# Strassen's algorithm on all columns of the down projection in groups 0 to 6 of an encoder's MLP

## The chip, the cores and the metric

The kernel runs on one core of a Trainium2 chip. The metric is the device time of one execution in microseconds; for the kernel before three runs gave 2014.59 to 2015.04, median 2015.0. Engines are named as the profile names them: PE is TensorE (PEld its weight loads), DVE is VectorE, ACT is ScalarE, POOL is GpSimd, SP is SyncE, whose queue issues the loads.

## The reference

Two layers of an encoder on 256 tokens of width 2048, all in float32. Each layer is RMSNorm, three attention mixers over one input projection, an output projection with residual, and then the part that the change touches, a squared-ReLU MLP of inner width 8192:

```python
for l in range(DEPTH):                       # DEPTH = 2
    ...                                      # mixers, output projection, residual
    h = rmsnorm(x, norm_mlp[l])
    u = jax.nn.relu(jnp.einsum('bsd,df->bsf', h, w_up[l]))        # 256 x 8192
    x = x + jnp.einsum('bsf,fd->bsd', u * u, w_down[l])           # 256 x 2048
return rmsnorm(x, norm_final)
```

## The kernel before, in words

**Numbers.** A float32 operand is split into a hi part (rounded to the matmul's input format, float32r) and a lo part (the rest). A product is hi x hi + lo x hi + hi x lo: three matmuls of 128 x 128 weights by 512 columns for each pair of blocks. The tiles of B that a step multiplies with are split on the way: ScalarE casts the hi tile (line 988, `whi`), VectorE subtracts it from the raw tile for the lo (line 989, `wlo`). There are three hi and three lo buffers, and two more (`spare`) that serve as a fourth hi and lo tile in some stages and hold B11 in the MLP.

**Steps.** All of the work on weights is one list of steps. A step has a tile of weights of 512 KB (1024 columns on 128 partitions), its load (issued 7 steps ahead, `LOOK_LOAD`), its split (2 or 3 steps ahead), sometimes sums of weight tiles (`prep`, 5 steps ahead), and its matmuls. A scheduler then puts the instructions of each engine in one fixed order, in which each waits for its operands, so that an instruction that waits holds up all that stand behind it on its engine.

**The MLP.** The 8192 rows of w_down are 8 groups of 1024. While group g goes down, group g+1 comes up: 16 up steps (4 blocks q of 4 steps, 8 matmuls of 512 columns and 8 of 256 each, lines 691 and 696). After each block, an evacuation (lines 668 to 676) adds halves, applies ReLU, scale and square, and splits the result; `sums_of` (lines 712 to 717) makes the sums of A that Strassen's products need.

**Strassen.** In groups 0 to 6 the left 1024 columns of w_down go by Strassen's algorithm in Winograd's form: A (the 256 tokens by 1024 rows) and B (1024 rows by 1024 columns) are 2 x 2 blocks, and seven products P1 to P7 take the place of eight. Each product is two steps of 6 matmuls (line 802), one for each half h of its rows. The products P1, P6, P5, P3 gather in bank a and P7, P4 in bank d of one pair tile `S` of PSUM, P2 in a bank of its own; after each product its bank is added to or subtracted from x (line 782). The sums of B that P6, P7 and P4 need are made by VectorE (lines 815, 817, 821, 832): 8 a group. The other 1024 columns go by plain steps of 12 matmuls (line 477), 8 a group, evacuated by line 739; group 7 is plain throughout. Between the two steps of a product stands an up or plain step, and between two products stand two or three.

Of the kernel before, what the change touches and what calls it, by code (L numbers as in the profile page):

```python
# [43 lines left out]
def tile_trunk(ctx: ExitStack, tc: tile.TileContext, x_in, w_in, w_o, w_up, w_down,  # L44
               gains, rowp, t5, rpb, gfin, cst, onehot, out):
    nc = tc.nc
    LOOK_LOAD, LOOK_SPLIT, LOOK_PREP, BUDGET = 7, 2, 5, 2.2
# [417 lines left out]
    class Step:  # L465


        def __init__(self, src, kk, n, pre, mm, fourth=True, loads=None, prep=None, raw=None, post=None):
            self.src, self.kk, self.n, self.pre, self.mm, self.fourth = src, kk, n, pre, mm, fourth
            self.loads, self.prep, self.raw, self.post = loads or [], prep, raw, post  # L470
# [33 lines left out]
    def layer_steps(l):  # L504
# [152 lines left out]
        def up_steps(g):  # L657

            out_, evacs = [], []
            for q in range(4 * g, 4 * g + 4):  # L660
                box = {}

                def evac(q=q, box=box):
                    need(("rrow", l))
                    a = mid(F32, 2, 256)
                    for i in range(2):

                        nc.scalar.copy(a[:, i, :], box["b"][i][:, 256:512])
                        nc.vector.tensor_add(a[:, i, :], a[:, i, :], box["b"][i][:, 0:256])
# [11 lines left out]
                for s in range(4):  # L681
# [19 lines left out]
                    out_.append(Step(w_up[l, q * 4 + s], 4, 256, pre, mm, fourth=False,  # L701
# [5 lines left out]
        def sums_of(q, a):  # L707
# [3 lines left out]
            a11, a21, a12 = v[:, 0, :], v[:, 1, :], v[:, 2, :]  # L711
            nc.vector.tensor_sub(sm[:, 0:2, :], v[:, 0:4:3, :], v[:, 1:2, :].to_broadcast([P, 2, P]))
            nc.vector.scalar_tensor_tensor(sm[:, 2, :], sm[:, 1, :], -1.0, a11, op0=ALU.mult, op1=ALU.subtract)
# [6 lines left out]
        def down_steps(g, js):  # L720
            out_ = []
            for j in js:
                box = {}
                for k in range(4):
                    def mm(wh, wl, j=j, k=k, box=box):
                        if k == 0:
# [3 lines left out]
                        hts = [uT[4 * g + k]] * 2  # L730
                        mode_b(box["b"], hts, wh, wl, [0, 1], k == 0, k == 3, blocks=(0,) if final else (0, 1),
                               lo_last=g < 7)
# [7 lines left out]
                        if final:  # L740
# [3 lines left out]
                            for c in range(2):  # L744
                                cols = slice(c * 256, c * 256 + 256)
                                for i, (hts, vh, vl) in enumerate(box["w"]):
                                    mode_b([None, tail[c]], hts, vh[:, :, cols], vl[:, :, cols], [0, 1],
                                           i == 0, i == 3, n=256, blocks=(1,))
# [9 lines left out]
                    out_.append(Step(w_down[l, (g * 4 + j) * 4 + k], 2, 512, None, mm, fourth=g == 7))  # L758
            return out_

        def strassen_steps(g):
# [5 lines left out]
            raw, t2, box = {}, {}, {}  # L767

            def src(par, j, h):
                return w_down[l, g * 16 + (par * 2 + j) * 2 + h]  # L770

            def left(name, q):

                if name[0] == "A":
                    t, kk = int(name[1]) - 1, int(name[2]) - 1
                    return [uT[q][:, i, kk, t * P:(t + 1) * P] for i in range(2)]
                return [sT[q][:, i, "3124".index(name[1]), :] for i in range(2)]

            def evac(bank, t, j, sign):
                xs = x[:, t, j * 512:(j + 1) * 512]  # L780
# [4 lines left out]
            plan = [("P1", "A11", "a", True, (0, 0, 1)), ("P6", "S2", "a", False, (1, 0, 1)),  # L785
                    ("P7", "S3", "d", True, (1, 1, -1)), ("P5", "S1", "a", False, (1, 1, -1)),
                    ("P3", "S4", "a", False, (0, 1, -1)), ("P2", "A12", "b", True, (0, 0, 1)),
                    ("P4", "A22", "d", False, (1, 0, 1))]
            out_ = []
            for name, lf, bk, fresh, dst in plan:  # L790
                for h in range(2):
                    def mm(wh, wl, name=name, lf=lf, bk=bk, fresh=fresh, dst=dst, h=h):
# [3 lines left out]
                        if (name, h) == ("P2", 0):  # L796
                            box["b"] = mm_bank()
                        o = box[bk]
                        ops = [left(lf, 2 * h + i + 4 * g) for i in range(2)]
                        for a, w in ((0, wh), (1, wh), (0, wl)):  # L800
                            for i in range(2):
                                nc.tensor.matmul(o, ops[i][a], w[:, i, :], skip_group_check=True,  # L802
                                                 start=fresh and h == 0 and i == 0 and a == 0 and w is wh,
                                                 stop=h == 1 and i == 1 and w is wl)
                        if h == 1:
# [369 lines left out]
```

## Time and profile before

| | |
|---|---|
| median of 3 runs | 2015.0 us (2014.59 to 2015.04) |
| the profiled execution | 2015.19 us, span 2013.4 us, mean clock 0.999 |
| busy: PE, DVE, ACT, POOL | 2000.6 us (99%), 1618.2 (80%), 1200.9 (60%), 290.6 (14%) |
| loads of w_down | 144 plain (`wraw`), 84 to `side`, 28 to `spare`, 512 KB each |
| transfer engines | 59.8% of their time on the loads' queue, mean 191 GB/s |

The profile is a record of one execution. A busy share is a mean over stages, and the MLP is about two thirds of the span, so the tables by stretches are read for it. A row of the timeline has the start, the duration, the engine, the line of the kernel, and tiles written <- tiles read. Durations of instructions that follow each other overlap a little, so the pace is read from their starts.

### The profile page before, as it was taken

The numbers are of one execution on the slowest core, as the hardware profiler recorded it, in microseconds if no ns is written. First come the engines' busy times: TensorE is split into PE (matmuls) and PEld (weight loads), VectorE is DVE, ScalarE is ACT, GpSimd is POOL, SyncE is SP. The second block draws the span as 40 slices with busy tenths as digits, with TensorE's granted clock in tenths as the row PEclk, the third lists the DMA queues.
The fourth block names the chain that finished last, engine by engine and source line by source line (L and its number), as shares of the span: only waits on it lengthen the run. The fifth ranks groups of instructions, "written<-read, shape, count | busy, mean of one in ns | idle before, by whom it ended". The sixth has DMA issues, their size and how long they took to land.

```text
span 2013.4 us, 27963 instructions
## 1 busy us (share of the span) xinstructions
PE 2000.6 (99%) x10264; PEld 1706.0 (85%) x10264; DVE 1618.2 (80%) x2112; ACT 1200.9 (60%) x1732; POOL 290.6 (14%) x336
## 2 busy tenths in 40 slices
PE   9999999999999999999999999999999999999998
PEld 7888888888888888888888888888888888888887
DVE  6677877879888898887657688778888888888875
ACT  6667756565555556555656677565655556555554
POOL 0684520000000000000008745100000000000001
PEclk9999999999999999999999999999999999999999
DMA  7745655565575656656666456555665756657554
GB/s 276 226 154 162 209 170 190 168 217 193 178 228 170 219 184 192 215 172 198 189 184 200 152 176 198 176 189 179 192 215 170 231 167 210 205 169 233 166 167 156
DMA packets 110102, 384.97 MB, mean 191 GB/s; under 512 B 12515, under 2 KB 16867, under 8 KB 109964
## 3 DMA queue, kind: packets, MB, share of 16 engines
q1 hardware_dynamic: 109532, 382.08, 59.8%
q8 instruction: 81, 1.33, 0.3%
q10 hardware_dynamic: 432, 1.10, 0.2%
q14 instruction: 57, 0.47, 0.1%
HBM read 377.34 MB, written 2.11 MB: 188 GB/s over the span
## 4 chain that ended last, share of the span: by engine, by line
PE 98%; ACT 1%; DVE 0%; issue 0%; DMA 0%; SPq 0%; DVEq 0%; POOLq 0%; POOL 0%
PE mm L477 44%; PE mm L691 23%; PE mm L696 12%; PE S L802 11%; PE mm L802 2%; PE tr L392 1%; PE tr L411 1%; PE S L355 1%; PE S L354 1%; PE tr L221 1%; PE tr L404 0%; ACT big L372 0%; PE tr L267 0%; DMA x<-in_x_dram 0%; PE tr L283 0%
## 5 line engine op out<-in xcount | busy, mean ns | idle before, releaser
L989 DVE TENSOR_TENSOR wlo<-wraw,whi 128x1024 fp32r<-128x1024 f32 (+1 forms) x531 | 654.6, 1236 | 212.5 <-ACT whi L988 209.9
L988 ACT CAST whi<-wraw 128x1024 fp32r<-128x1024 f32 (+1 forms) x531 | 556.7, 1051 | 418.1 <-PE mm L691 170.2
L477 PE MATMUL mm<-whi,big 128*128 128x512 f32 (+1 forms) x2252 | 643.8, 386 | 0.5 <-ACT whi L988 0.5
L691 PE MATMUL mm<-big,whi 128*128 128x512 f32 x2048 | 509.5, 391 | 0.0
L477 PEld LDWEIGHTS mm<-whi,big 128*128 128x128 f32 x2252 | 418.6, 188 | 83.5 <-ACT whi L988 2.5
L691 PEld LDWEIGHTS mm<-big,whi 128*128 128x128 f32 x2048 | 377.1, 188 | 74.1
L477 PE MATMUL mm<-wlo,big 128*128 128x512 f32 (+1 forms) x1126 | 374.9, 384 | 0.0
L696 PEld LDWEIGHTS mm<-big,wlo 128*128 128x128 f32 x2048 | 279.4, 190 | 20.0
L696 PE MATMUL mm<-big,wlo 128*128 128x256 f32 x2048 | 285.5, 282 | 0.0
L477 PEld LDWEIGHTS mm<-wlo,big 128*128 128x128 f32 x1126 | 211.8, 188 | 39.6
L802 PE MATMUL S<-whi,big 128*128 128x512 f32 x672 | 182.2, 393 | 0.0
L477 PE MATMUL mm<-spare,big 128*128 128x512 f32 (+1 forms) x678 | 157.8, 381 | 0.0
L988 ACT CAST whi<-side 128x1024 fp32r<-128x1024 f32 x84 | 88.2, 1050 | 95.2 <-PE mm L691 77.8
L477 PEld LDWEIGHTS mm<-spare,big 128*128 128x128 f32 x678 | 122.3, 188 | 23.2
L802 PEld LDWEIGHTS S<-whi,big 128*128 128x128 f32 x672 | 119.1, 189 | 18.7
L989 DVE TENSOR_TENSOR wlo<-side,whi 128x1024 fp32r<-128x1024 f32 x84 | 102.7, 1223 | 37.5 <-ACT whi L988 37.1
L257 POOL TENSOR_TENSOR sm<-sm,mhalf 128x2 f32<-128x2 f32 (+2 forms) x14 | 15.3, 1092 | 793.7 <-DVE sm L252 773.9
L988 ACT CAST whi<-big 128x1024 fp32r<-128x1024 f32 x56 | 59.0, 1053 | 85.1 <-DVE big L817 36.4
L870 POOL TENSOR_TENSOR x<-x,big 128x512 f32<-128x512 f32 x6 | 8.6, 1451 | 669.5 <-ACT mid L877 669.5
L802 PE MATMUL S<-wlo,big 128*128 128x512 f32 x336 | 103.9, 390 | 0.0
L383 POOL TENSOR_SCALAR big<-big,sm 128x256 f32<-128x256 f32 x128 | 90.3, 723 | 3.0
L989 DVE TENSOR_TENSOR spare<-wraw,spare 128x1024 fp32r<-128x1024 f32 x54 | 70.2, 1299 | 22.2 <-ACT spare L988 21.7
(151 smaller groups left out, 2081.3 us busy)
## 6 DMA issues: line engine op xcount, KB each, us to landing
wraw<-in_w_up_dram SPq DMA_DIRECT2D x256, 512.0 KB, 4.1
wraw<-in_w_down_dram SPq DMA_DIRECT2D x144, 512.0 KB, 3.7
wraw<-in_w_in_dram SPq DMA_DIRECT2D x119, 512.0 KB, 3.8
side<-in_w_down_dram SPq DMA_DIRECT2D x84, 512.0 KB, 4.2
wraw<-in_w_o_dram SPq DMA_DIRECT2D x64, 512.0 KB, 3.6
spare<-in_w_down_dram SPq DMA_DIRECT2D x28, 512.0 KB, 4.2
side<-in_rpb_dram SPq DMA_DIRECT2D x32, 174.8 KB, 5.1
side<-avec SPq DMA_DIRECT2D x8, 384.0 KB, 5.4
```

The source lines that it names most:

```text
L221: tr = nc.tensor.transpose(psv[:, kk, t, :], x[:, t, c0:c0 + P], ident).ins
L354: nc.tensor.matmul(o, st, u.kh[:, kh, :], start=True, stop=False)
L355: nc.tensor.matmul(o, st, u.kl[:, kh, :], start=False, stop=True)
L383: nc.gpsimd.tensor_scalar(p[:, s, :], p[:, s, :], rs[:, s:s + 1], 1.0, op0=ALU.mult, op1=ALU.mult)
L392: nc.tensor.transpose(ps[:, c * P:(c + 1) * P], u.p[:, s, kb * P:(kb + 1) * P], ident)
L411: nc.tensor.matmul(ps, u.V[:, kb, u.kv, :, :], pt[:, kb, :], start=n == 0, stop=n == 3)
L477: return nc.tensor.matmul(banks[t][:, 0:n], a, (wl if part == "hl" else wh)[:, i, :], start=first and i == 0 and part == "hh", stop=last a ...
L691: nc.tensor.matmul(box["b"][fs], wh[:, kk, fs * P:(fs + 1) * P], ht, start=s == 0 and kk == 0, stop=False, skip_group_check=True)
L696: nc.tensor.matmul(box["b"][fs][:, 0:256], wl[:, kk, fs * P:(fs + 1) * P], ht[:, 0:256], start=False, stop=s == 3 and kk == 3, skip_group_ ...
L802: nc.tensor.matmul(o, ops[i][a], w[:, i, :], skip_group_check=True, start=fresh and h == 0 and i == 0 and a == 0 and w is wh, stop=h == 1 ...
L988: act = nc.scalar.copy(h[:, part], w[:, part]).ins
L989: last_lo[0] = nc.vector.tensor_sub(lo[:, part], w[:, part], f(h[:, part])).ins
```

## The change

All 2048 columns of groups 0 to 6 go by Strassen's algorithm, as two halves of 1024. A half has 14 steps of 6 matmuls, so a group has 28 of them and 16 up steps, with no plain step. The order of steps is one Strassen step, one up step, one Strassen step for each product, with two up steps ahead of a group and one more between the halves.

- The order of products is P1, P2, P7, P6, P5, P3, P4. P2 of each half has a PSUM bank of its own for the whole layer (`own`), gathers over the groups and is evacuated after group 6 alone.
- B11 is loaded into a plain buffer (`wraw`, five of them) and stays there. B12 is then added onto it by an accumulating transfer from GpSimd's queue (`on_top`, line 796), where VectorE added before; B21 is added onto t2 in the same way. B21 itself is the plain load of P2's step. VectorE keeps two sums for each half of rows: B12 + B22 (line 828) and t2 = B22 + B11 (line 833).
- The `spare` tiles are the fourth hi and lo tile in all stages (every fourth step), and up and Strassen steps are split up to 3 steps ahead (`ahead=4`), the others 1.
- The evacuation of an up block writes its halves in another order, so that the three blocks of A that the products use as they are lie side by side, and 384 columns are split where 512 were.

```diff
-        def __init__(self, src, kk, n, pre, mm, fourth=True, loads=None, prep=None, raw=None, post=None):
+        def __init__(self, src, kk, n, pre, mm, ahead=2, loads=None, prep=None, raw=None, post=None):
...
-                    u = big(F32R, 2, 2, 256)
-                    nc.scalar.copy(u[:, 0], a)
-                    nc.vector.tensor_sub(u[:, 1], a, f(u[:, 0]))
+                    u = big(F32R, 2, 512)
+                    n, af = 384 if q < 28 else 512, a.rearrange("p k c -> p (k c)")
+                    nc.scalar.copy(u[:, 0, 0:n], af[:, 0:n])
+                    nc.vector.tensor_sub(u[:, 1, 0:n], af[:, 0:n], f(u[:, 0, 0:n]))
...
-            plan = [("P1", "A11", "a", True, (0, 0, 1)), ("P6", "S2", "a", False, (1, 0, 1)),
-                    ("P7", "S3", "d", True, (1, 1, -1)), ("P5", "S1", "a", False, (1, 1, -1)),
-                    ("P3", "S4", "a", False, (0, 1, -1)), ("P2", "A12", "b", True, (0, 0, 1)),
+            plan = [("P1", "A11", "a", True, (0, 0, 1)), ("P2", "A12", "b", True, (0, 0, 1)),
+                    ("P7", "S3", "d", True, (1, 1, -1)), ("P6", "S2", "a", False, (1, 0, 1)),
+                    ("P5", "S1", "a", False, (1, 1, -1)), ("P3", "S4", "a", False, (0, 1, -1)),
                     ("P4", "A22", "d", False, (1, 0, 1))]
+
+            def on_top(tile, par, j, h):
+                nc.gpsimd.dma_start(tile, src(par, j, h).rearrange("p (k n) -> p k n", k=2), accum_op=ALU.add)
...
-                        if h == 1:
+                        if h == 1 and (bk != "b" or g == 6):
                             evac(o, *dst)
                     loads, prep, get = [], None, None
                     if name == "P1":
-                        loads = [(("B11", h), src(0, 0, h), lambda h=h: spare(F32, h))]
+                        loads = [(("B11", h), src(0, 0, h), lambda: wp.tile([P, 2, 512], F32, tag="wraw", bufs=5, name=nm("b11")))]
                         get = lambda h=h: raw["B11", h]
+                    elif name == "P2":
+                        def prep(h=h):
+                            assert ("P1", h) in done
+                            on_top(raw["B11", h], 0, 1, h)
...
                         def prep(h=h):
-                            nc.vector.tensor_add(raw["B11", h], raw["B11", h], raw["B12", h])
                             t2[h] = big(F32, 2, 512)
                             nc.vector.tensor_add(t2[h], raw["B22", h], raw["B11", h])
                         get = lambda h=h: t2[h]
...
+                    elif name == "P5":
+                        def prep(h=h):
+                            assert ("P6", h) in done
+                            on_top(t2[h], 1, 0, h)
                         get = lambda h=h: raw["B11", h]
...
-            ss = down_steps(g, (2, 3)) + up_steps(g + 1)
-            hs = strassen_steps(g)
+            ss = up_steps(g + 1)
+            hs = strassen_steps(g, 0) + strassen_steps(g, 1)
             order = [0, 0]
-            for p_ in range(7):
-                order += [1, 0, 1] + ([0, 0] + [0] * (p_ in (1, 3, 5)) if p_ < 6 else [])
+            for p_ in range(14):
+                order += [1, 0, 1] + [0] * (p_ == 6) if p_ < 13 else [1, 1]
...
-        if s.fourth and fourth[0] % 4 == 0:
+        if i % 4 == 3:
...
-        while ns < min(len(steps), i + LOOK_SPLIT + (not s.fourth)):
+        while ns < min(len(steps), i + s.ahead):
```

What this makes of each engine's order is shown at two places. First PE, at the end of one product and the start of the next that waits for an evacuation, in a middle group of the first layer. Before, P7's last step (`S_4610`) and the start of the two up steps that stand between it and P5, whose first row waits for P7's evacuation:

```order
L802 MATMUL S_4610<-whi_4799,big_4416 128x512
L802 MATMUL S_4610<-whi_4799,big_4548 128x512
L802 MATMUL S_4610<-wlo_4800,big_4416 128x512 [waits DVE_49]
L802 MATMUL S_4610<-wlo_4800,big_4548 128x512
L691 MATMUL mm_4779<-big_3321,whi_4809 128x512 [waits Activation_49]
L691 MATMUL mm_4780<-big_3321,whi_4809 128x512
```

Now, in the second half of a group (`S_7353`), P7's last step (`whi_7449`) and P6's first (`whi_7461`):

```order
L810 MATMUL S_7353<-whi_7449,big_6870 128x512
L810 MATMUL S_7353<-wlo_7450,big_6672 128x512 [waits DVE_49]
L810 MATMUL S_7353<-wlo_7450,big_6870 128x512
L810 MATMUL S_7353<-whi_7461,big_6285 128x512 [waits DVE_49,Activation_49]
L810 MATMUL S_7353<-whi_7461,big_6483 128x512
L810 MATMUL S_7353<-whi_7461,big_6285 128x512
L810 MATMUL S_7353<-whi_7461,big_6483 128x512
L693 MATMUL mm_7479<-big_3237,whi_7473 128x512 [waits Activation_49]
```

The first row of P6 waits for VectorE, and the instruction that it waits for is P7's evacuation; nothing stands between the two products any more.

Second VectorE at the same two places. Before, the evacuation (L782) of P7 and what stands ahead of it:

```order
L989 TENSOR_TENSOR wlo_4776<-wraw_4706,whi_4775 128x1024 [waits DMAHW6_49,Activation_49]
L832 TENSOR_TENSOR big_4626<-side_4992,big_4626 128x1024 [waits DMAHW3_49]
L989 TENSOR_TENSOR wlo_4800<-side_4617,whi_4799 128x1024 [waits PE_49,Activation_49]
L989 TENSOR_TENSOR wlo_4810<-wraw_4736,whi_4809 128x1024 [waits DMAHW7_49,PE_49,Activation_49]
L989 TENSOR_TENSOR wlo_4832<-wraw_4754,whi_4831 128x1024 [waits DMAHW0_49,PE_49,Activation_49]
L832 TENSOR_TENSOR big_4660<-side_5043,big_4660 128x1024 [waits DMAHW5_49]
L782 TENSOR_TENSOR x<-x,S_4610 128x512 [waits PE_49]
L989 TENSOR_TENSOR wlo_4845<-spare_4478,whi_4844 128x1024 [waits Activation_49]
```

Now, from the evacuation of an up block (`mid_7432`) to P7's (L786) and the lo tile of P6's first step (`wlo_7462`):

```order
L669 TENSOR_TENSOR mid_7432<-mid_7432,mm_7292 128x256 [waits Activation_49]
L670 SCALAR_TENSOR_TENSOR mid_7432<-mid_7432,rrow 128x512 [waits DVE_49]
L714 TENSOR_TENSOR mid_7442<-mid_7432 128x256 [waits Activation_49]
L715 SCALAR_TENSOR_TENSOR mid_7442<-mid_7442,mid_7432 128x128 [waits DVE_49]
L678 TENSOR_TENSOR big_7439<-mid_7432,big_7439 128x384 [waits Activation_49]
L716 SCALAR_TENSOR_TENSOR mid_7442<-mid_7442,mid_7432 128x128 [waits DVE_49]
L828 TENSOR_TENSOR side_7732<-side_7732,side_7734 128x1024 [waits DMAHW6_49,DMAHW0_49]
L719 TENSOR_TENSOR big_7446<-mid_7442,big_7446 128x512 [waits Activation_49]
L833 TENSOR_TENSOR big_7453<-side_7347,b_1416_7221 128x1024 [waits DMASW4_49]
L833 TENSOR_TENSOR big_7477<-side_7385,b_1426_7273 128x1024 [waits DMASW5_49]
L786 TENSOR_TENSOR x<-x,S_7353 128x512 [waits PE_49]
L1002 TENSOR_TENSOR wlo_7462<-big_7453,whi_7461 128x1024 [waits Activation_49]
```

The rows ahead of the evacuation were lo tiles for steps further on and sums for P4; now the sums for P6 (L833, which wait for the accumulating transfers, `DMASW`) and a sum for the next half's P7 (L828) stand ahead of the evacuation.

More of the change, by code (lines that the diff above doesn't have):

```diff
@@ L699, in mm @@
                             evac()
-                    out_.append(Step(w_up[l, q * 4 + s], 4, 256, pre, mm, fourth=False,
+                    out_.append(Step(w_up[l, q * 4 + s], 4, 256, pre, mm, ahead=4,
                                      post=evacs[0] if (q, s) == (1, 0) else None))
@@ L718, in sums_of, with down_steps @@
             sT[q] = t
-        def down_steps(g, js):
+        def down_steps(g):
             out_ = []
-            for j in js:
+            for j in range(4):
                 box = {}
```

83 lines of the change are left out of this document (40 added, 43 removed).

## The prediction

> **What bounds the kernel now.** I read the page's busy shares and the chain that ended last, then one group of the MLP in the table by stretches, then the timelines of TensorE, VectorE and ScalarE inside a group, and last the landing times of transfers.
>
> ```profile
> PE 2000.6 (99%) x10264; PEld 1706.0 (85%) x10264; DVE 1618.2 (80%) x2112; ACT 1200.9 (60%) x1732; POOL 290.6 (14%) x336
> ...
> PE 98%; ACT 1%; DVE 0%; issue 0%; DMA 0%; SPq 0%; DVEq 0%; POOLq 0%; POOL 0%
> ```
>
> TensorE (PE) is the bound: it is never idle and holds 98% of the chain. Shares over the whole kernel hide the stage that changes, so here are two groups, cut from the first matmul of the same Strassen product in one group to that in the next:
>
> ```profile
> core 0: us, PE busy (x) PEld busy (x) DVE busy (x) ACT busy (x) POOL busy (x), PEclk, DMA share, GB/s
> 530.37:615.87 85.50, 85.50 (x439) 73.12 (x438) 73.67 (x89) 49.16 (x59) 0.00 (x0) 1.00 0.62 197
> 615.87:701.36 85.49, 85.49 (x439) 73.11 (x437) 73.68 (x89) 49.16 (x59) 0.00 (x0) 1.00 0.61 197
> ```
>
> A group lasts 85.5 us, and VectorE (DVE) works 73.7 of them. So a group has 11.8 us of VectorE slack, and that is the stock from which this change pays. The clock is granted in full, GpSimd (POOL) does nothing there.
>
> **What PE saves.** The pace of its steps, by starts in the timeline:
>
> ```profile
> 736.86 1.09 PE L802 MATMUL S<-whi,big 128*128 128x512 f32 x4
> 737.79 0.62 PE L802 MATMUL S<-wlo,big 128*128 128x512 f32 x2
> 738.25 1.98 PE L691 MATMUL mm<-big,whi 128*128 128x512 f32 x8
> 740.07 1.12 PE L696 MATMUL mm<-big,wlo 128*128 128x256 f32 x8
> 741.02 1.09 PE L802 MATMUL S<-whi,big 128*128 128x512 f32 x4
> ...
> 742.40 1.98 PE L691 MATMUL mm<-big,whi 128*128 128x512 f32 x8
> 744.22 1.12 PE L696 MATMUL mm<-big,wlo 128*128 128x256 f32 x8
> 745.17 2.00 PE L691 MATMUL mm<-big,whi 128*128 128x512 f32 x8
> ```
>
> A Strassen step (6 matmuls) takes 738.25 - 736.86 = 1.39 us, an up step 745.17 - 742.40 = 2.77 us. The changed group has 28 Strassen and 16 up steps: 28 x 1.39 + 16 x 2.77 = 83.2 us, 2.3 less than 85.5. By matmuls it is 12 fewer a group, and a plain step of 12 without a seam takes 2.72 us:
>
> ```profile
> 1006.86 2.88 PE L477 MATMUL mm<-spare,big 128*128 128x512 f32 x12
> 1009.58 0.39 PE L477 MATMUL mm<-whi,big 128*128 128x512 f32 x1
> ```
>
> Over 14 groups that is 32 to 38 us; I take 35.
>
> **What VectorE gains in work.** Its pace, by starts where it did not wait:
>
> ```profile
> 706.98 0.75 DVE L669 TENSOR_TENSOR mid<-mid,mm 128x256 f32<-128x256 f32 x2
> 707.64 0.68 DVE L782 TENSOR_TENSOR x<-x,S 128x512 f32<-128x512 f32 x1
> 708.24 0.69 DVE L670 SCALAR_TENSOR_TENSOR mid<-mid,rrow 128x512 f32<-128x512 f32 x1
> ...
> 711.88 0.42 DVE L712 TENSOR_TENSOR mid<-mid 128x256 f32<-128x256 f32 x1
> 712.22 1.22 DVE L815 TENSOR_TENSOR spare<-spare,side 128x1024 f32<-128x1024 f32 x1
> 713.35 0.29 DVE L713 SCALAR_TENSOR_TENSOR mid<-mid,mid 128x128 f32<-128x128 f32 x1
> 713.55 1.22 DVE L989 TENSOR_TENSOR wlo<-spare,whi 128x1024 fp32r<-128x1024 f32 x1
> 714.69 0.28 DVE L714 SCALAR_TENSOR_TENSOR mid<-mid,mid 128x128 f32<-128x128 f32 x1
> ```
>
> So 1024 columns take 1.14 us, 512 take 0.60, 256 take 0.33, 128 take 0.20; 384 is then about 0.47. A group's lo subtractions go from 38 to 44 (+6.8 us), its evacuations into x from 11 to 12 (+0.6; P2 stays in its own bank until group 6), its sums of B stay at 8 (two halves would need 16, but 8 are now accumulating transfers), and four up evacuations split 384 columns for 512 (-0.5). VectorE needs 73.7 + 6.9 = 80.6 us in a group of 83.2: its slack shrinks from 11.8 to 2.6 us. ScalarE gets 6 casts more, about 6 us on 49.2: no bound.
>
> **Where it hits.** An average of 97% leaves no room for a local heap, and the order has one. Before, the shortest PE work between a product's last matmul and the next one that waits for its evacuation is 5.4 us (two plain steps), everywhere. Now it is 2.8 us or less at most such places, and none at all where P6 follows P7 in the second half (12 of the 14 groups); there P6 waits for P7's evacuation although it writes the other bank of the pair, as the row of P6 in the built order says. I walk VectorE's queue there, from the end of the up step that stands ahead of P2's second step (0 us). PE has P2, P7, up, P7: 3 x 1.39 + 2.77 = 6.94 us until P6. VectorE has, in its order: one lo (0.2 to 1.34, after its cast), the two L669 and L670 (2.6), then a wait for ScalarE's square,
>
> ```profile
> 708.91 1.06 ACT L988 CAST whi<-wraw 128x1024 fp32r<-128x1024 f32 x1 [1.22 <-PE mm L477]
> 709.87 0.72 ACT L673 ACTIVATE mid<-mid,zero 128x512 f32<-128x512 f32 x1
> ```
>
> 0.72 us (3.5), then L714, L715, L678, L716 (0.33 + 0.2 + 0.47 + 0.2, with their handovers: 4.75), the sum for the next P7 (L828, 5.9), L719 (6.5), both sums for P6 (L833, 7.6 and 8.8), and only then P7's evacuation (9.4, written at 9.5). P6 waits for it: 9.5 - 6.94 = 2.6 us of idle PE. L828 can make it longer. The B22 tile that it reads is loaded once the lo at 1.34 is done, so from 1.5 us, and lands so much later:
>
> ```profile
> side<-in_w_down_dram SPq DMA_DIRECT2D x84, 512.0 KB, 4.2
> ...
> big<-in_gfin_dram SPq DMA_DIRECT2D x2, 512.0 KB, 6.1
> ```
>
> At 5.7 us, where VectorE stands ready at 4.75: 0.95 more, 3.5 in all. The same late load is there before, at the sum for P4, and cost VectorE 1.2 us a time (30.8 by 26), in its slack:
>
> ```profile
> DVE big L832 <- DMA side<-in_w_down_dram: 30.8, 26, 2.2
> ```
>
> The bounds are 2.6 (landed in 3.2 us or less) and 5.5 (landing like the slowest 512 KB row); I take 3.2, nearer the side row, since no other load is queued just ahead of this one. 12 x 3.2 = 38 us.
>
> In the first half an up step lies between P7 and P6, so PE arrives at 3 x 1.39 + 2 x 2.77 = 9.71. VectorE has also the lo of that up step, which waits for its cast, and P7's evacuation ahead of P6's sums: L828 at 5.4 to 5.8, first L833 done at 8.8 to 9.2, its cast at 9.9 to 10.3 (0.2 to 0.6 late), second L833 at 10.6, the lo of P6 at 11.7, where PE wanted it at 9.71 + 0.93 = 10.64. So 1.1 us; and VectorE, then three lo subtractions behind, writes P6's evacuation some 0.6 us after PE has run out of cover for P5. From 0 (if VectorE is that much quicker) to 2.2; I take 1.7, x 14 = 24 us. The other crossings (P5 to P3, P3 to P4, P4 to P1) come out within cover by the same walk: 0, and 14 us if each missed by 0.25 us twice a half.
>
> **What I cost at nothing.** SP issues 32 loads a group as before. The plain buffers: two of five hold B11 for some 15 steps, so some loads are issued only 3.2 us of PE work ahead of their cast. ScalarE then waits about 1 us, and the 4 hi and lo tiles (up to three steps, 5.5 us of PE work) hide it; without that cover 14 x 1 = 14 us. The accumulating transfers (112, GpSimd's queue): the sum for P6 has 14 us of PE work between issue and use, t2 for P4 has 7.6 us in the first half, 9.5 in the second. No row shows one; the bounds are 4.2 us, a plain load, and 8.4, a load and a read of the same size: 0 to 14 x 0.8 = 11 us. I take 0, as they run in a stage where the transfer engines are 0.62 busy; with 40 transfers for 32 they would be 0.75, with double price 0.9.
>
> **The sum**, against the profiled execution (2015.19 us, of which the span is 2013.4; the median of the runs is 2015.0): 2015.2 - 35 + 38 + 24 = **2042 us**.
>
> **A rule beside a row.** One VectorE form with two SBUF inputs runs in the attention stage, where GpSimd works too, and takes from 469 to 1518 ns for the same shape:
>
> ```profile
> L435 DVE SCALAR_TENSOR_TENSOR big<-mid,gn,big x32: 469/960/1518, 108.3 to 1284.2; 128x256 fp32r<-128x256 f32 x32
> ```
>
> The Trainium skill, "SBUF — State Buffer", section "Who interferes with whom", says that such an instruction contends with GpSimd's reads of SBUF and infers that making the descriptors of a GpSimd DMA needs only the write interface. By that the accumulating transfers start freely and VectorE is not slowed, the sum stays; no run here has shown such a transfer. Were descriptors held by subtractions, it would be the third case below.
>
> **The rivals.** (1) PE stays the bound and the saving is kept: 1980 us. For it: the chain is 98% PE, and the table by stretches leaves VectorE 2.6 us of slack. Against: the walk, whose 2.6 us a group needs no late transfer. The half-way form, the second half's floor alone, gives 2015 - 38 + 31 = 2008. (2) Walk right in place, but the crossings of the first half cost nothing: 2018. Against it: the lo of P6 has seven VectorE instructions and two casts ahead of it in 9.7 us. (3) Accumulating transfers land late: from 7.6 us on, the cast for P4 stands at the head of ScalarE's queue, all later hi tiles behind it, and PE runs out. At 10 us 14 x 2.4 + 14 x 0.5 = 41 more: 2083. For it: GpSimd's queue is new and both sides of the sum are moved; against it: only the rows of plain loads.
>
> **Chances.** The forecast with its sizes (2024 to 2070) 0.60; case 1 with its half-way form, faster than 2011, 0.15; case 2 with its neighbourhood, 2011 to 2024, 0.13; case 3, over 2070, 0.12. About 0.2% (4 us) is what this kernel's measurement can tell from no change: faster 0.15, same 0.08, slower 0.77. The range of 8 in 10 leaves out most of case 1 and the far end of case 3: 2011 to 2080.
>
> **What would show it.** PE idle some 3 us once a group ahead of the Strassen matmuls, with the evacuation into x (VectorE) as releaser; group periods of 86 to 89 us; VectorE's share in the group near 0.9, not 0.97; L828 waiting for its load twice a group, half a us to one us. Wrong would be: PE at 99% and periods near 83.2 (case 1); VectorE or ScalarE waiting for GpSimd's transfers (case 3); VectorE subtractions far over 1.22 us in the MLP (the rule fails).

## The result and the profile after

The change makes the kernel slower by 7.3%: median 2161.7 us (2155.7 to 2169.2, 4 runs) against 2014.9, ratio 1.0731 (95% interval 1.0718 to 1.0743). The forecast was 2042 us in a range of 2011 to 2080: the direction came, but the loss of 147 us is more than five times the 27 that were forecast. The profiled execution has a span of 2153.9 us, 140.5 more than before.

The page of the changed kernel: busy times, transfer queues (packets, MB, share of the 16 engines' time), and the chain that ended last:

```profile
PE 2026.9 (94%) x10096; PEld 1704.6 (79%) x10096; DVE 1715.2 (80%) x2214; ACT 1267.7 (59%) x1816; POOL 392.4 (18%) x448
...
q1 hardware_dynamic: 109532, 382.08, 51.9%
q0 software_dynamic: 16128, 58.73, 15.7%
...
PE 72%; DMA 12%; DVE 10%; ACT 3%; issue 2%; DVEq 0%; ACTq 0%; POOLq 0%; POOL 0%
```

Two numbers of this page hold the whole loss. PE is idle for 2153.9 - 2026.9 = 127.0 us, 114.2 more than before (12.8). And PE is busy for 26.3 us *more* than before, although it has some 35 us less to do. The second is the clock: its mean went from 0.999 to 0.970, which is 64.6 us of full speed lost in 2153.9. The chain, 98% PE before, now runs 25% through transfers, VectorE and ScalarE.

Two groups by stretches, each cut from the same evacuation in one group to that in the next:

```profile
core 0: us, PE busy (x) PEld busy (x) DVE busy (x) ACT busy (x) POOL busy (x), PEclk, DMA share, GB/s
499.84:597.06 97.22, 87.88 (x426) 73.40 (x425) 80.46 (x98) 53.88 (x65) 6.98 (x8) 0.95 0.72 213
597.06:694.44 97.38, 88.87 (x425) 74.08 (x425) 80.54 (x97) 53.95 (x65) 6.99 (x8) 0.93 0.73 221
```

A group takes 97.3 us where the forecast had 86 to 89. VectorE's work in it is 80.5 us, the 80.6 of the prediction. Idle time of PE is some 9 us a group, in two places: ahead of P6 in each half. The clock is 0.93 to 0.95 of full. In the groups of the page (busy, mean ns of one, then idle time before and what ended it) the second half's pauses stand in the first row, the first half's in the second:

```profile
L810 PE MATMUL S<-whi,big 128*128 128x512 f32 x1064 | 309.2, 414 | 65.4 <-DVE x L786 65.4
L810 PE MATMUL S<-spare,big 128*128 128x512 f32 x420 | 125.4, 437 | 43.2 <-ACT spare L1001 36.2
```

This is the chain of waits up to the pause in the second half of a group (start, us, what):

```profile
512.49 1.14 DVE wlo L1002
513.63 1.15 DVE spare L1002
...
514.79 8.37 DMA wraw<-in_w_up_dram
...
523.25 1.06 ACT spare L1001
...
525.48 1.22 DVE wlo L1002
...
526.73 4.43 DMA side<-in_w_down_dram
...
531.18 1.23 DVE side L828
532.41 0.60 DVE big L719
533.01 2.27 DVE big L833 x2
535.28 0.61 DVE x L786
...
536.02 2.04 PE S L810 x4
```

PE ran out of work at 529.89. Read backwards, P6 (536.02) waits for P7's evacuation (L786), this for the two sums of P6 (L833), these for L828, which waits for a B22 tile that landed at 531.16. That tile could not be loaded before a lo subtraction at 525.48, and this stood in VectorE's queue behind the lo tile of an up step whose load took **8.37 us** to land. What was in flight beside that load (timeline):

```profile
509.85 0.87 POOL L796 DMA_DIRECT2D b<-in_w_down_dram  x1 [17.62 <-DVE wlo L1002]
511.05 0.33 SPq L989 DMA_DIRECT2D wraw<-in_w_down_dram  x1
513.93 0.87 POOL L796 DMA_DIRECT2D b<-in_w_down_dram  x1 [3.21 <-DVE wlo L1002]
514.79 4.77 SPq L989 DMA_DIRECT2D wraw<-in_w_up_dram  x3
```

The second accumulating transfer was issued 0.86 us before the load. Over the kernel the landing times (median, us) are:

```profile
wraw<-in_w_up_dram SPq DMA_DIRECT2D x256, 512.0 KB, 6.2
...
side<-in_w_down_dram SPq DMA_DIRECT2D x112, 512.0 KB, 4.8
wraw<-in_w_down_dram SPq DMA_DIRECT2D x88, 512.0 KB, 5.0
...
b<-in_w_down_dram SPq DMA_DIRECT2D x56, 512.0 KB, 7.9
b<-in_w_down_dram POOLq DMA_DIRECT2D x56, 512.0 KB, 7.1
big<-in_w_down_dram POOLq DMA_DIRECT2D x56, 512.0 KB, 7.6
```

The up loads went from 4.1 to 6.2 us. By the queue rows a MB costs the 16 engines 51.9% of 16 x 2153.9 us / 382.08 = 46.8 us as a plain load and 15.7% of the same / 58.73 = 92.1 us as an accumulating transfer, 1.97 times as much.

Behind the pauses the clock falls. In the same table by stretches (columns as above) the first row is the 6.8 us behind the pause of the first half, the others a stretch without a pause, the pause of the second half, and what follows it:

```profile
488.06:494.88 6.82, 6.82 (x18) 5.18 (x19) 6.79 (x7) 4.94 (x5) 1.74 (x2) 0.57 0.46 71
503.47:529.89 26.42, 26.42 (x136) 22.17 (x134) 21.83 (x30) 14.52 (x20) 1.74 (x2) 1.00 0.84 255
529.89:536.02 6.13, 0.00 (x0) 0.03 (x1) 5.25 (x8) 2.40 (x3) 0.00 (x0) 0.91 0.03 13
536.02:542.85 6.83, 6.83 (x22) 5.53 (x23) 5.54 (x5) 3.81 (x5) 1.74 (x2) 0.58 0.61 118
```

PE is busy throughout 488.06 to 494.88 and gets through 18 matmuls at a granted clock of 0.57. The prediction had no such term.

### The profile page after: what moved, and what is told of

The parts are those of the page before. It is cut to its first block, busy times and chain, and to the rows that moved or that the text cites. A ratio compares the mean times of both kernels' runs of the same rounds, so it can differ in the third digit from the quotient of the medians.

```text
span 2153.9 us, 28285 instructions
## 1 busy us (share of the span) xinstructions
PE 2026.9 (94%) x10096; PEld 1704.6 (79%) x10096; DVE 1715.2 (80%) x2214; ACT 1267.7 (59%) x1816; POOL 392.4 (18%) x448
## 3 DMA queue, kind: packets, MB, share of 16 engines
q1 hardware_dynamic: 109532, 382.08, 51.9%
q0 software_dynamic: 16128, 58.73, 15.7%
## 4 chain that ended last, share of the span: by engine, by line
PE 72%; DMA 12%; DVE 10%; ACT 3%; issue 2%; DVEq 0%; ACTq 0%; POOLq 0%; POOL 0%
PE mm L477 26%; PE S L810 18%; PE mm L693 15%; PE mm L698 7%; DMA wraw<-in_w_up_dram 6%; DMA side<-in_w_down_dram 5%; DVE wlo L1002 3%; DVE big L833 2%; DVE side L828 1%; PE tr L392 1%; ACT spare L1001 1%; PE mm L810 1%; DVE spare L1002 1%; DVE x L786 1%; PE tr L411 1%
## 5 line engine op out<-in xcount | busy, mean ns | idle before, releaser
L1002 DVE TENSOR_TENSOR wlo<-wraw,whi 128x1024 fp32r<-128x1024 f32 (+1 forms) x383 | 473.3, 1242 | 193.3 <-ACT whi L1001 169.8
L1001 ACT CAST whi<-wraw 128x1024 fp32r<-128x1024 f32 (+1 forms) x383 | 400.4, 1049 | 273.0 <-PE mm L477 83.4
L477 PE MATMUL mm<-whi,big 128*128 128x512 f32 (+1 forms) x1356 | 422.5, 384 | 0.3 <-ACT whi L1001 0.2
L810 PE MATMUL S<-whi,big 128*128 128x512 f32 x1064 | 309.2, 414 | 65.4 <-DVE x L786 65.4
L477 PEld LDWEIGHTS mm<-whi,big 128*128 128x128 f32 x1356 | 250.6, 188 | 48.2 <-ACT whi L1001 2.2
L1002 DVE TENSOR_TENSOR spare<-wraw,spare 128x1024 fp32r<-128x1024 f32 x146 | 182.7, 1252 | 103.4 <-ACT spare L1001 94.6
L477 PE MATMUL mm<-wlo,big 128*128 128x512 f32 (+1 forms) x678 | 255.4, 381 | 0.0
L1001 ACT CAST spare<-wraw 128x1024 fp32r<-128x1024 f32 x146 | 153.3, 1050 | 160.0 <-DMA wraw<-in_w_down_dram 37.7
L810 PE MATMUL S<-spare,big 128*128 128x512 f32 x420 | 125.4, 437 | 43.2 <-ACT spare L1001 36.2
L1002 DVE TENSOR_TENSOR wlo<-b,whi 128x1024 fp32r<-128x1024 f32 x112 | 136.9, 1223 | 18.0 <-ACT whi L1001 17.1
L1001 ACT CAST whi<-b 128x1024 fp32r<-128x1024 f32 x112 | 117.1, 1047 | 57.5 <-PE mm L693 49.1
```

The costliest lines, as they stand in the source:

```text
L477: return nc.tensor.matmul(banks[t][:, 0:n], a, (wl if part == "hl" else wh)[:, i, :], start=first and i == 0 and part == "hh", stop=last a ...
L1001: act = nc.scalar.copy(h[:, part], w[:, part]).ins
L1002: last_lo[0] = nc.vector.tensor_sub(lo[:, part], w[:, part], f(h[:, part])).ins
```

## The experiments

Four theories. **A**: the accumulating transfers load the transfer engines, so that other loads land late. **B**: VectorE's total work is the floor, whatever the order. **C**: each pause brings a stretch of half clock. **E** (D is its first form): the order around P6's sums is what is wrong. All runs, with PE's idle time (span less busy time) and mean clock of the profiled execution:

| run | median us | ratio to before (95%) | PE idle us | clock |
|---|---|---|---|---|
| the change | 2161.7 | 1.0731 (1.0718 to 1.0743) | 127.0 | 0.970 |
| e1 no transfers | 2092.0 | 1.0373 (1.0347 to 1.0398) | 79.1 | 0.984 |
| e2 transfers without addition | 2118.8 | 1.0522 (1.0502 to 1.0541) | 98.4 | 0.975 |
| e3 zero matmuls, both halves | 2196.9 | 1.0903 (1.0885 to 1.0921) | 99.8 | 0.984 |
| e4 other order of steps | 2127.4 | 1.0563 (1.0538 to 1.0588) | 110.6 | 0.979 |
| e5 next sum behind P6's | 2099.8 | 1.0421 (1.0399 to 1.0443) | 92.2 | 0.984 |
| e6 two tiles for the banks | 2153.3 | 1.0671 (1.0645 to 1.0697) | 128.5 | 0.968 |
| e7 = e5 + e6 | 2055.3 | 1.0200 (1.0168 to 1.0232) | 67.1 | 0.991 |
| e8 zero matmuls, second half | 2139.3 | 1.0622 (1.0605 to 1.0638) | 87.2 | 0.982 |
| e9 sums 6 steps ahead | 2050.7 | 1.0181 (1.0154 to 1.0209) | 61.6 | 0.992 |
| e10 = e7 + e9 | 2021.0 | 1.0029 (1.0015 to 1.0042) | 39.6 | 0.997 |
| e11 = e10, half the transfers by GpSimd's adds | 2098.8 | 1.0414 (1.0397 to 1.0432) | 85.7 | 0.993 |
| e12 = e10, half the transfers by VectorE's adds | 2030.0 | 1.0073 (1.0057 to 1.0089) | 45.8 | 0.997 |
| e13 = e10 without transfers | 1980.1 | 0.9827 (0.9814 to 0.9839) | 13.7 | 0.999 |
| e14 = e9 + P7's steps adjacent | 2007.3 | 0.9966 (0.9954 to 0.9977) | 27.8 | 0.998 |
| e15 = e10 + four products adjacent | 2009.0 | 0.9968 (0.9960 to 0.9977) | 33.0 | 0.999 |

### The transfers: left out (e1), and without their addition (e2)

```diff
-                nc.gpsimd.dma_start(tile, src(...), accum_op=ALU.add)
+                return                                   # e1
+                nc.gpsimd.dma_start(tile, src(...))      # e2
```

> The 112 accumulating transfers are left out, so B12 is missing from the sums for P6 and P5 and B21 from the one for P4; all else stands. Theory A (the transfers load the transfer engines, other loads land later, and VectorE's sums start later): the up loads land at about 4.1 us again (6.2 with the transfers), the pauses ahead of P6 shrink from 5.4 to about 3 us in the second half and from 3.1 to under 2 in the first, and fewer of them are followed by a half clock: 2040 to 2085 us. Theory B (VectorE's own queue is too long ahead of P6, whatever lands when): pauses and time stay, 2130 us or more.

> The same transfers on GpSimd's queue without the addition: B12 takes the place of B11 and B21 that of t2, so the sums are wrong in value and the waits the same. Theory A with its price (an accumulating transfer costs the engines about double, 92 against 47 us of engine time for each MB): half of what the transfers cost goes, 2085 to 2125 us, landing of these transfers some 4 to 5 us for 7.2. If GpSimd's queue (issue and waits) is what costs, nothing changes: 2150 us or more.

Without the transfers 70 us of the 147 go. The up loads land in 3.7 us (page of e1):

```profile
PE 2010.7 (96%) x10096; PEld 1690.4 (81%) x10096; DVE 1717.0 (82%) x2214; ACT 1270.8 (61%) x1816; POOL 295.0 (14%) x336
...
L810 PE MATMUL S<-whi,big 128*128 128x512 f32 x1064 | 302.0, 407 | 50.3 <-DVE x L786 50.3
...
L810 PE MATMUL S<-spare,big 128*128 128x512 f32 x420 | 114.7, 404 | 16.2 <-ACT spare L1001 8.8
...
wraw<-in_w_up_dram SPq DMA_DIRECT2D x256, 512.0 KB, 3.7
```

But 79 us of idle time stay. In the first layer the first half's pause shrinks to single waits of 0.4 to 1.5 us, and the second half's is still 3.6 to 5.2 (2.9 to 5.2 over both layers). The time is 7 us over the range that A gave, so A holds for about half of the loss, and the rest has another cause. With the addition gone but the transfers kept, 43 us go; the up loads land in 4.5. So of the 70 us some 43 belong to the addition and 27 to 112 more transfers of any kind.

### The clock: PE kept busy in the pauses (e3, e8)

```diff
+                        if (name, h) == ("P6", 0) and g < 6:
+                            for _ in range(FILL[half]):      # (10, 20) in e3, (0, 14) in e8
+                                nc.tensor.matmul(own[half], warm[:, 0:P], warm, skip_group_check=True,
+                                                 start=False, stop=False)
```

> In groups 0 to 5, ahead of P6, PE gets 10 (first half) or 20 (second half) matmuls with a zero operand added into P2's bank: 2.3 and 4.5 us of work that would have been idle. Theory C (each pause of some 2 us or more is followed by one or two stretches of 3.4 us at half clock, 123 us in all, which cost 61): the pauses shrink to about 1 us, the half clock goes, 12 pieces of 14 groups: 2105 to 2120 us. If the clock drops for another reason, or the added matmuls come late themselves: 2150 us or more.

> Only in the second half of groups 0 to 5, ahead of P6, 14 matmuls with a zero operand (3.2 us) are added into P2's bank; they stand where PE idled 5.4 us, so they delay nothing that waits for PE by itself. Theory C (a pause is followed by a half clock): the half clocks at 12 places of about 5 us go, each worth half its length: 2130 to 2150 us. If the clock does not cost what the records say, or the added work delays the rest as in the run with 10 and 20: 2160 us or more.

e3 is a miss: 35 us slower, where 40 to 60 faster were expected. Its 360 matmuls are some 82 us of work (by e8's pace, 3.2 us for 14), and PE's idle time fell by 27 alone. The half clock did go behind the filled pauses of the second half, but the added work stands ahead of steps on which later casts, lo tiles and loads wait, and a pause appeared where none had been (timeline of e3, an up step waiting for its lo tile):

```profile
554.67 1.98 PE L693 MATMUL mm<-big,whi 128*128 128x512 f32 x8
559.85 1.73 PE L698 MATMUL mm<-big,wlo 128*128 128x256 f32 x8 [3.20 <-DVE wlo L1006]
```

So the pause cannot be treated as free time of PE: what ends it depends, through released buffers, on what PE did before. In e8 the added 3.2 us stand only at the end of P7 in the second half, where nothing but P6 follows:

```profile
528.11 3.36 PE L810 MATMUL mm<-warm 128*128 128x512 f32 x14
532.80 1.17 PE L814 MATMUL S<-whi,big 128*128 128x512 f32 x4 [1.33 <-DVE x L786]
533.85 0.72 PE L814 MATMUL S<-wlo,big 128*128 128x512 f32 x2
```

P6 then starts at full pace (1.05 us for four matmuls; 536.02 to 537.87 in the change). The time falls by 22 us with 38 us of useless work added. PE idles 39.8 us less, about what was added, and is busy 20.5 us more (2047.4) for the 38 us of work: the 18 us between the two are clock. The mean clock rose from 0.970 to 0.982, which is 26 us of full speed. So C holds for these pauses.

### The order of steps (e4)

```diff
-                order += [1, 0, 1] + [0] * (p_ == 6) if p_ < 13 else [1, 1]
+                order += [1, 1, 0] + [0] * (p_ == 6) if p_ < 13 else [1, 1]
```

> The order of steps is product, product, up in place of product, up, product: 2.77 us of PE work stand between P7 and P6 in both halves, but only 1.4 at P6 to P5 and P5 to P3 in the second. Theory D (the place P7 to P6 is the trouble): the second half's pause falls from 5.4 to 2.6 us, less often with a half clock: 2090 to 2115 us. Theory B (VectorE is behind by a queue that moves on to the next crossing): the pause comes back at P5 or P3, 2140 us or more.

34 us faster, short of what D expected. The pause at P7 to P6 in the second half did fall to about 2 us, but others came (2.4 us between two Strassen steps that wait for a hi tile, 0.6 at an up step). Inconclusive between D and B by itself: cover moved to one crossing is missing at others.

### VectorE's order, and the wait for the wrong bank (e5, e6, e7)

```diff
                         def prep(h=h):                       # P7
-                            nc.vector.tensor_add(raw["B12", h], raw["B12", h], raw["B22", h])
+                            with tc.issue_after(last_t2[0]) if last_t2[0] else ExitStack():   # e5, e7
+                                nc.vector.tensor_add(raw["B12", h], raw["B12", h], raw["B22", h])
...
-        return pp.tile([P, 4, 256], F32, tag="S", bufs=1, name=nm("S"))
+        return [pp.tile([P, 2, 256], F32, tag="S" + e, bufs=1, name=nm("S" + e)) for e in "ad"]   # e6, e7
```

> VectorE's sum for the next half's P7 (B12 + B22) is put behind the two sums for this half's P6; nothing else. Theory E (in the order as built that sum stands ahead of P6's sums, though its product comes some 15 steps later, and waits for its late load): the 2.1 us from 531.2 to 533.0 in the trace (a wait of 0.9 and the sum itself) leave the way to P6 in the second half, 3 us in the first; pauses 5.4 and 3.1 fall to about 3 and under 1.5 us, half clocks with them: 2080 to 2115 us. Rival (transfers and VectorE's total work set the pace, in whatever order): 2140 us or more.

> Banks a and d are two tiles in place of a pair, so P6 waits for P7's evacuation no more (nor P4 for P3's); the attention's row maxima of one kind are taken in two halves. By the prediction's step (the evacuation of P7 behind the sums is the floor) the pause ahead of P6 in the second half goes and the time falls under 2110 us. By the trace of the change (the hi tile of P6 itself is cast at 534.2 to 535.3, behind the same sums, and the evacuation is written at 535.9) only some 0.6 us a pause go: 2135 to 2155 us.

> Both edits: the sum for the next P7 behind P6's sums, and two tiles for banks a and d. If the order of VectorE and the wait for the wrong bank hide each other: 2040 to 2075 us, less than either alone by more than their sum. If transfers that load the engines set the rest, no lower than 2085.

e5 alone gives 62 us, e6 alone 8, both 106, 36 more than their sum. One side of the reason shows in e6: with the wait for the evacuation gone, the pause is nearly as long as before and has another releaser, the hi tile of P6, which is cast from the same late sums (timeline of e6):

```profile
531.05 2.35 DVE L833 TENSOR_TENSOR big<-side,b 128x1024 f32<-128x1024 f32 x2
532.36 1.04 ACT L1001 CAST whi<-big 128x1024 fp32r<-128x1024 f32 x1 [3.47 <-DVE big L833]
533.45 2.08 PE L810 MATMUL Sa<-whi,big 128*128 128x512 f32 x4 [5.82 <-ACT whi L1001]
```

So the evacuation that the profile names as releaser was the last of two waits that ended within 1 us of each other; the cause stood ahead of both, in the order around P6's sums. The other side shows in e5 in the first half, where the pauses did not fall (42.2 us by this row of its page for 43.2, where under 1.5 each was expected): their releaser was P6's hi tile and is now P7's evacuation.

```profile
L810 PE MATMUL S<-spare,big 128*128 128x512 f32 x420 | 119.5, 424 | 42.2 <-DVE x L786 42.2
```

Once the order is mended so far, the wait for the wrong bank is worth 45 us (2099.8 to 2055.3). One limit of e5: its gain is in the second half, and there, with L828 behind P6's sums, the scheduler also put an up step between P7 and P6, where nothing stood. So e5 shows that the order there matters, not which of the two moves gave how much; the order as a whole gets its number below, from e1 and e13.

### One number (e9), and all three edits (e10)

```diff
-    LOOK_LOAD, LOOK_PREP, BUDGET = 7, 5, 2.2
+    LOOK_LOAD, LOOK_PREP, BUDGET = 7, 6, 2.2
```

> One number: sums of B and accumulating transfers are recorded 6 steps ahead in place of 5, so VectorE's order has P6's sums earlier against lo tiles and evacuations. Theory E (what is wrong is the place of the sums in VectorE's order): the pause ahead of P6 in the second half falls below 2 us, 2030 to 2080 us. If the transfers and VectorE's total work set the pace: over 2120.

> Two tiles for the banks, the next P7's sum behind P6's, and 6 steps for 5. The order is mended as far as these three go and the transfers stay. Theory A+E (the order takes one part, the transfers the other): 2010 to 2045 us, with the loads still landing in about 6 us. If the order was all: below 2000 us.

Recording sums and accumulating transfers one step earlier takes 111 of the 147 us. The second half's pauses come to 0.6 to 2.3 us, a few over the 2 that were expected. The edit also issues the transfers a step earlier; how much of the 111 is theirs was not tried. With e7's edits it comes to 2021 us, 0.3% over the kernel before, with every transfer kept. B falls as the explanation of the loss: VectorE's work is 79.4 us in a group of 84.8 and was 80.5 in one of 97.2 (a group of e10 by stretches, columns as above):

```profile
484.30:569.10 84.80, 83.55 (x426) 70.52 (x425) 79.42 (x97) 54.10 (x65) 6.98 (x8) 1.00 0.84 247
```

### B11 + B12 by GpSimd (e11) or VectorE (e12) in place of a transfer

```diff
-                            on_top(raw["B11", h], 0, 1, h)                                   # P2
+                            nc.gpsimd.tensor_add(raw["B11", h], raw["B11", h], raw["B12", h])   # P7, e11; nc.vector in e12
```

> As the run with all three edits, but B11 + B12 is added by GpSimd from the B12 tile that is in SBUF anyway, in place of the accumulating transfer: 56 transfers remain. An addition of 128x1024 takes GpSimd some 2.7 us (twice the 1.35 us of 128x512 in the attention). Theory A (transfers): 1980 to 2010 us, up loads land near 5 us. Rival (VectorE's subtractions are slowed while GpSimd adds, as L435 from 469 to 1518 ns in the attention): VectorE's L1002 goes well over 1.25 us in the mean and the time stays at 2020 or more.

> As that run, but VectorE makes B11 + B12: 4 additions of 1.14 us a group more on VectorE, 80.6 + 4.6 = 85.2 us for the 83.2 of PE. If VectorE's total is the floor, a group cannot take less than 85.2: 2015 to 2035 us. If the transfers were worth more than VectorE's slack, it is still faster than the run with all three edits.

With half of the transfers the up loads land in 4.1 and 3.9 us (5.4 in e10), yet both are slower than e10. In e11 the gain is eaten by GpSimd and VectorE slowing each other. Here are its 56 additions among the groups by line of e11 (mean ns of one behind the busy time):

```profile
L828 POOL TENSOR_TENSOR b<-b,side 128x1024 f32<-128x1024 f32 x56 | 176.6, 3153 | 585.5 <-DVE wlo L1004 379.3 <-DVE mid L717 165.8 <-DMA wraw<-in_w_up_dram 40.4
```

The groups by line of VectorE in e11 have L720 at 1322 ns, a form that takes 687 in the change:

```profile
L720 DVE TENSOR_TENSOR big<-mid,big 128x512 fp32r<-128x512 f32 x56 | 74.0, 1322 | 0.0
```

And a group of e11 by stretches has 86.6 us of VectorE and PE idle for 5.3:

```profile
493.56:584.85 91.29, 86.00 (x423) 69.65 (x422) 86.61 (x98) 53.73 (x64) 16.41 (x8) 1.00 0.67 204
```

VectorE's busy time in the kernel rises from 1702.0 us (e10) to 1808.9, by 1.9 us for each of the 56 additions; an addition on VectorE itself costs 1.07 (1761.8 in e12). The rival of e11 held, with a price far over what was given for it: of the 107 us the lo subtractions, by which it was to be known, took some 39 (1.28 us in the mean for 1.23 in e10), sums of A such as L720 most of the rest. In e12 a group takes 86.2 us with 83.6 of VectorE, as B would have it; PE is busy for 83.5 of it too, so that VectorE's total is the floor there is not shown.

### What the transfers cost where the order leaves cover (e13)

Left out as in e1, in the kernel of e10.

> The run with all three edits (two tiles, the next P7's sum behind, sums 6 steps ahead; 2021 us), with the 112 accumulating transfers left out, so that B12 and B21 are missing from the sums. Theory A+E (transfers cost much only where the order leaves no cover; here a pause of 1.25 us a group and 25 us of pauses in all are left): 1980 to 2000 us, 20 to 40 less, against the 70 that leaving them out was worth in the unmended order. If the transfers cost the same 70 in any order: below 1960. If what is left is VectorE's total alone: within 6 us of 2021.

The page of e13, its busy times and its chain:

```profile
PE 1964.6 (99%) x10096; PEld 1672.0 (85%) x10096; DVE 1705.8 (86%) x2230; ACT 1276.4 (65%) x1816; POOL 291.8 (15%) x336
...
PE 97%; DMA 1%; ACT 1%; DVE 1%; issue 0%; SPq 0%; DVEq 0%; POOLq 0%; POOL 0%; ACTq 0%
```

And a group of e13 by stretches:

```profile
482.26:565.12 82.86, 82.86 (x426) 70.69 (x425) 79.69 (x98) 54.55 (x65) 0.00 (x0) 1.00 0.61 202
```

1980.1 us: the time of the prediction's first rival, which kept the whole saving of 35 us. A group takes 82.9 us (83.2 predicted) and PE is never idle in it. Between this and e10 lie the transfers: 41 us, just over the 20 to 40 expected. With e1 that makes a square: the order costs 112 us without transfers (2092.0 - 1980.1) and 141 with them, the transfers 41 in the mended order and 70 in the other. Each makes the other dearer by 29 us.

### Two versions that beat both kernels (e14, e15)

```diff
-    LOOK_LOAD, LOOK_PREP, BUDGET = 7, 5, 2.2
+    LOOK_LOAD, LOOK_PREP, BUDGET = 7, 6, 2.2
...
-                order += [1, 0, 1] + [0] * (p_ == 6) if p_ < 13 else [1, 1]
+                order += ([1, 1, 0] if p_ in (2, 9) else [1, 0, 1]) + [0] * (p_ == 6) if p_ < 13 else [1, 1]
```

That is e14; e15 has e7's edits too, and (2, 5, 9, 11) for (2, 9).

> Two numbers of the change: sums and transfers 6 steps ahead for 5, and P7's two steps next to each other with the up step behind them, so that 2.77 us of PE work stand between P7 and P6 in both halves by the order itself. Theory E: the pause ahead of P6 goes: 2000 to 2030 us, from 2051 with the first of the two. If VectorE's total is the floor, no better than 2045.

> The three edits, and in the order of steps the two of P7 next to each other in both halves, P3's in the first and P5's in the second, each with its up step behind: the evacuation of P6 that ended the 1.25 us pause once a group gets more cover. Theory E: what is left of the pauses (25 us) goes by half or more: 1995 to 2012 us, faster than before the change. Rival (VectorE has 80.6 us of work in 83.2 and loads that come 1 to 2 us late, so another place takes over): 2015 to 2030 us.

Two small edits of the change make it 0.34% faster than the kernel before, by 7.8 us; e15's interval lies inside e14's, so its further edits are worth nothing that can be measured. A group of e14 by stretches:

```profile
481.75:565.54 83.79, 83.50 (x426) 70.52 (x425) 79.69 (x97) 54.30 (x65) 6.98 (x8) 1.00 0.84 251
```

PE is down to 0.3 us of idle time in this one. What is left to e13 is 27 us; the transfers keep the engines 0.84 busy, and loads land in 5.4 us in the median. How those 27 us split was not tried.

## Why the prediction was wrong

- **PE saves 35 us: right.** e13 shows it nearly alone: busy time of PE 2000.6 to 1964.6, 36.0.
- **VectorE needs 80.6 us a group: right** (80.5). That this alone would leave room was not claimed, and e13 with 79.7 in 82.9 shows that it can.
- **The two places: right.** The pauses are ahead of P6, in the second half with P7's evacuation as releaser, in the first with the tiles of P6. Elsewhere PE hardly waits.
- **Their sizes: wrong, and this is the first step that failed.** The second half's pause was put at 3.2 us and is 5.4 (12 places, 4.8 to 6.9); the first half's 1.7, and it is 2.9 (14 places). Together 106 us for 62. The walk started at the end of the up step ahead of P2's second step with a lo tile "0.2 to 1.34". In the trace that point is 522.83 and the lo tile comes at 525.48, 2.65 after it for 0.2: the up step's load, not in the walk, took 8.37 us. From there the walk repeats itself: evacuation written 13.1 us after the start for 10.4 with L828's late load, 2.7 later. The walk priced L828's own load (0.95) and took every load ahead of it as landed. That they were not is the transfers' doing: without them (e1) the same places come to 63 us, 47 in the second half for 38 forecast and 16 in the first for 24. That the two misses there cancel to 1 us is luck, but for the order alone the walk's pauses are of the right size.
- **Accumulating transfers at nothing: wrong.** They were watched for landing late themselves (7.1 and 7.6 us in the median, within the bounds of 4.2 to 8.4, 9.8 at most; no wait in the profile ends with one, so their own cover held, as assumed). What they did was make the *other* loads late. The engines' share was given as 0.75 to 0.9, and the price of double as a bound; the trace has 1.97 times. But the plain loads kept their landing times of before in the sum. The transfers were 70 us of the 147; in the profiled executions of the change and e1, 48 of idle PE and 16 of its busy time.
- **No term for the clock: the second step that failed.** 64.6 us at full speed were lost to it by the mean clock, 2.0 before. By the records of the granted clock, 24 stretches of 3.4 or 6.8 us ran at one half between 391 and 1993 us. The Trainium skill, "TensorE: Matmul & The Clock Gate", section "Part 1: The HAM clock gate (the "warmup" mystery)", says that PE goes to half speed after an idle window of about 3.4 us and back after a busy one. The trace agrees on the half and on the length of the stretches, but by that rule a pause of 3.2 us, as forecast, need not have cost any clock, and here the measurement decides: 43 of 47 pauses of 3.0 to 3.8 us came with a half clock. The forecast's own pauses had this price: without the transfers, with 63 us of pauses, PE is busy for 46 us more than in e13 (2010.7 - 1964.6).
- **The sum with what was measured:** 2015.2 - 35 + 106 for the pauses + 62 for the clock (busy time of PE, 2026.9 - 1964.6) = 2148, and the profiled execution has 2155.7. The 62 of the clock and the 44 more of pauses are the miss, and of the 62 some 46 stay without the transfers.
- **The releaser was taken for the cause.** The prediction held the wait for P7's evacuation, in the other bank, to be the floor of the second half. e6 took it away and gained 8 us. What set the time was the order around P6's sums (e5, e9); the walk had those rows and priced their waits, but took the last row of the chain for its cause.
- **Rivals.** Case 3 (accumulating transfers) is nearest in time and had 0.12; its mechanism, ScalarE waiting for a late t2, is not what happened. Case 1 is what the change does without its transfers and with three edits of its order.
- **The rule held.** In the change 158 of the subtractions of L1002 run while GpSimd issues one of its 112 transfers, and none of these takes over 1229 ns. In e11, where GpSimd reads SBUF, 21 of those of L1004 take 2.8 to 3.4 us, each beside one of its additions. The Trainium skill, "SBUF — State Buffer", section "Who interferes with whom", has both, the first as an inference. What the transfers did to other loads was the price.

## What to carry to other kernels

A pause of the bounding engine is priced with what follows it: here 106 us of pauses brought another 62 at half clock. When a change adds transfers, the first question is not whether they land in time but what each load that shares the engines with them does, and which instruction in front of the critical one reads such a load. And before a costly layout is given up, it pays to read the order of the queue that ends the pause: two small edits that place sums and steps turned 7.3% slower into 0.34% faster.

## What the runs showed of the hardware that was not expected

- Pauses well under 3.4 us, the length of the shortest half-clock stretch, can halve the clock. Over the 17 profiles here, from 300 us on, a half clock ran beside the pause or began within 2 us behind it for 3 of 70 pauses of 1.0 to 1.5 us, 31 of 94 from 1.5 to 2.2, 44 of 69 from 2.2 to 3.0, 43 of 47 from 3.0 to 3.8, and all 53 longer ones. Five of these were already at half clock when the pause began.
- An accumulating transfer of 512 KB costs the transfer engines 1.97 times a plain load (92.1 and 46.8 us for each MB), and without the addition the same queue costs 49.0 (8.5% of 16 x 2118.3 us for 58.73 MB in e2). It lands in 7.1 to 7.6 us in the median, no later than the plain B11 loads in the same groups, 7.9 us.
- One addition of 128x1024 on GpSimd takes 2.4 to 4.1 us beside VectorE's work and lengthens this by 1.9 us (e11), more than the addition costs on VectorE (1.07, e12).
